# Three layer boundaries of a two-block transformer kernel: the last products by column halves, squares summed unscaled, transposes ahead of the last products, high passes ahead of low passes

## The chip, the cores and the metric

The kernel runs on one core of a Trainium2 chip. The metric is device microseconds (us) of one execution. Five engines each work through their own list of instructions in order and meet at semaphores: TensorE (PE, matrix products and transposes into PSUM), VectorE (DVE), ScalarE (ACT), GpSimd (POOL) and SyncE (SP, which issues transfers).

## The reference

Two blocks run one after the other on 256 tokens of width 1024, in float32.

```python
u  = rms_norm(x, ln1) * (1 + scale1) + shift1        # block 1
x  = x + gate1 * (merged @ w_o)                      # convolution and state-space mixers
u2 = rms_norm(x, ln2) * (1 + scale2) + shift2
x  = x + gate2 * (square(relu(u2 @ w_up)) @ w_down)
x  = rms_norm(x, final_norm)
h  = rms(x, ln1_g) * (1 + sc1) + sh1                 # block 2
x  = x + g1 * (attention(h) @ w_out)
h2 = rms(x, ln2_g) * (1 + sc2) + sh2
x  = x + g2 * ((silu(h2 @ w_gate) * (h2 @ w_up)) @ w_down)
```

Three times a product into the width 1024 is followed by gate, residual, normalization over the whole row, scale and shift, and the next product: after `w_o`, after `w_down` of block 1 (there with `final_norm` in between) and after `w_out`. These places are the boundaries b1, b2 and b3.

## The kernel before

Each float32 matrix is held as two parts, high and low (`wh`, `wl` for weights, `hs`, `ls` for activations), and a product is the sum of three passes: high by high, high by low, low by high. Weights come in units of 1 MB, loaded some units ahead; ACT writes the high part (L133), DVE the low part (L141). In the long stages between the boundaries PE runs nearly without a gap. A scheduler orders the instructions there; inside `boundary` the order is that of the code (`tc.manual_schedule`), and a few of the scheduler's instructions are slipped in between.

The tokens are two tiles of 128, `t` = 0 and 1. A boundary has these steps, for each tile. `last(t, i)` are the last two units (`i`) of the product, 12 products of 512 columns each, into two PSUM banks, one for each half `c` of the columns. `res` multiplies by the gate (`rtmp`), adds to the residual `x`, and at b2 multiplies by `final_norm` (`xq`); `sq` is a sum of squares on ACT (two at b2); `stat` forms the mean on DVE in small steps and the power -1/2 on POOL (`rs`); `norm` scales each half (`xn`). `tf` transposes 8 blocks of 128 by 128 on PE into two PSUM banks of four blocks each; `mod` applies scale and shift to each block, four by ACT and four by DVE, into `f`; `high` and `low` (ACT, DVE) split pairs of blocks. `first(t, i)` are the products of the first two units of the next layer with these parts. `split_by_hand` splits one more weight unit in quarters.

The PSUM tile `tf` has two buffers (`aux`), which `hidt`, the transposes that follow b1 and b3, also use. Where ACT and DVE both read blocks of one bank, the program makes each read wait for the one before it.

After b2 the stage of attention begins: `fgps` and `fgsum` are two small products, `dk` is the next weight unit, and `qt` transposes `qn`, the normalized `dq`, whose chain runs ACT, DVE, POOL (`qkr`, L234), DVE (L1348).

## Time and profile before

| | |
|---|---|
| median of 3 runs | 936.97 us (936.65 to 939.52) |
| the profiled execution | 938.36 us, of which its trace spans 935.9 us |
| PE busy | 898.3 us of the span (96%) |
| DVE, ACT, POOL busy | 732.7, 516.9, 75.7 us |
| b1, b2, b3 in the trace | about 401 to 430, 590 to 625, 729 to 758 us |

The profiled execution is 1.39 us above the median of the runs. Rows of the trace give a start, a duration, an engine, a line, the operation with the tiles written and read, and in brackets the idle time before it and what ended that.

### The profile page before, as it was taken

The page shows a single profiled execution, that of the slowest core. Times are in us where ns is not written, and L with a number is a line of the kernel's source. Part 1 is how long each engine was busy: PE and PEld are TensorE (multiplying, and loading weights), DVE is VectorE, ACT ScalarE, POOL GpSimd, SP SyncE. Part 2 cuts the span into 40 slices and gives each one's busy share as a digit, 9 for nine tenths or more (in the row PEclk, how much of TensorE's full clock was granted, in tenths as well). Part 3 has the DMA queues.
Part 4 walks back from the last instruction along what each step waited for, and adds up shares of the span by engine and source line. Part 5 has one row for each costly group of instructions (what it writes and reads, how often), then busy time and mean ns, then how long its engine had stood idle before and what let it go on. Part 6 is the DMA issues. An engine that isn't in the chain of part 4 may idle for free.

```text
span 935.9 us, 14692 instructions
## 1 busy us (share of the span) xinstructions
PE 898.3 (96%) x5820; PEld 792.6 (85%) x5820; DVE 732.7 (78%) x1091; ACT 516.9 (55%) x901; POOL 75.7 (8%) x98
## 2 busy tenths in 40 slices
PE   5999999999999999989999999889899899999997
PEld 4899999999999999879888888667676698888886
DVE  4779779899989986669798898776878586666663
ACT  5465476676767754437444455465566475555441
POOL 5000000100110000010100100122220100000001
PEclk9999999999999999999999999989999999999999
DMA  9977999677857674556699799346333265655511
GB/s 340 353 254 243 316 354 321 203 262 257 309 195 263 225 250 155 181 202 231 233 356 350 252 360 342 126 134 212 136 118 124 87 212 193 188 203 187 188 46 45
DMA packets 124345, 210.72 MB, mean 225 GB/s; under 512 B 5581, under 2 KB 96045, under 8 KB 119029
## 3 DMA queue, kind: packets, MB, share of 16 engines
q1 hardware_dynamic: 121700, 202.16, 62.1%
q0 software_dynamic: 2496, 7.61, 2.4%
q8 instruction: 45, 0.74, 0.3%
q14 instruction: 24, 0.19, 0.1%
q10 hardware_dynamic: 80, 0.02, 0.0%
HBM read 208.67 MB, written 1.11 MB: 224 GB/s over the span
## 4 chain that ended last, share of the span: by engine, by line
PE 47%; DVE 4%; ACT 2%; POOL 1%; issue 1%; DVEq 0%; ACTq 0%; POOLq 0%
PE tmacc L1009 17%; PE up L682 5%; PE upj L682 3%; PE up L685 2%; PE gatej L682 2%; PE up2j L682 2%; PE gate L682 2%; PE upj L685 1%; POOL qkr L234 1%; PE fv L1273 1%; PE gatej L685 1%; PE gate L685 1%; PE up2j L685 1%; PE dq L1273 1%; PE gu L1189 1%; PE up L1189 1%
## 5 line engine op out<-in xcount | busy, mean ns | idle before, releaser
L141 DVE TENSOR_TENSOR wl<-raw,wh 128x1024 fp32r<-128x1024 f32 x264 | 315.3, 1220 | 75.4 <-ACT wh L133 75.3
L133 ACT ACTIVATE wh<-raw 128x1024 fp32r<-128x1024 f32 x264 | 267.3, 1052 | 138.8 <-PE tmacc L1009 18.4
L283 DVE SCALAR_TENSOR_TENSOR adaacc<-raw,ccol,adaacc 128x1024 f32<-128x1024 f32 x80 | 99.6, 1277 | 5.2 <-DMA raw<-in_w_ada_dram 5.2
L1009 PE MATMUL tmacc<-wh,hidh 128*128 128x512 f32 x216 | 67.2, 392 | 0.0
L1009 PE MATMUL tmacc<-wl,hidh 128*128 128x512 f32 x216 | 66.7, 390 | 0.0
L1009 PE MATMUL tmacc<-wh,hidl 128*128 128x512 f32 x216 | 66.6, 390 | 0.0
L682 PE MATMUL up<-fs,wh 128*128 128x512 f32 x192 | 48.6, 393 | 0.0
L1009 PEld LDWEIGHTS tmacc<-wl,hidh 128*128 128x128 f32 x216 | 40.6, 188 | 8.7
L1009 PEld LDWEIGHTS tmacc<-wh,hidl 128*128 128x128 f32 x216 | 40.5, 188 | 8.7
L1009 PEld LDWEIGHTS tmacc<-wh,hidh 128*128 128x128 f32 x216 | 38.8, 189 | 7.3 <-issue 0.8
L682 PEld LDWEIGHTS up<-fs,wh 128*128 128x128 f32 x192 | 35.1, 188 | 8.4 <-issue 1.7
L817 DVE SCALAR_TENSOR_TENSOR cv<-xc,cwx,cv 128x255 f32<-128x255 f32 (+2 forms) x96 | 39.6, 478 | 0.3 <-ACT cv L812 0.2
L926 PE MATMUL ssmacc<-yl,wh 128*128 128x256 f32 x128 | 35.7, 284 | 0.1
L926 PE MATMUL ssmacc<-yh,wl 128*128 128x256 f32 x128 | 35.7, 284 | 0.0
L926 PE MATMUL ssmacc<-yh,wh 128*128 128x256 f32 x128 | 34.4, 288 | 1.1 <-ACT yh L894 1.1
L701 PE MATMUL xs<-u,wh 128*128 128x256 f32 x256 | 34.6, 286 | 0.0
L701 PE MATMUL z<-u,wh 128*128 128x256 f32 x256 | 34.3, 284 | 0.0
L701 PE MATMUL gl<-u,wh 128*128 128x256 f32 x256 | 33.8, 284 | 0.0
L701 PEld LDWEIGHTS gl<-u,wh 128*128 128x128 f32 x256 | 31.9, 192 | 0.3 <-issue 0.3
L701 PEld LDWEIGHTS z<-u,wh 128*128 128x128 f32 x256 | 32.1, 192 | 0.0
L701 PEld LDWEIGHTS xs<-u,wh 128*128 128x128 f32 x256 | 32.0, 192 | 0.0
L682 PE MATMUL upj<-fs,wh 128*128 128x512 f32 x112 | 28.1, 393 | 0.0
(438 smaller groups left out, 1964.5 us busy)
## 6 DMA issues: line engine op xcount, KB each, us to landing
raw<-in_w_in_dram SPq DMA_DIRECT2D x50, 1024.0 KB, 5.1
raw<-in_w_ada_dram SPq DMA_DIRECT2D x40, 1024.0 KB, 5.6
raw<-in_w_up_dram SPq DMA_DIRECT2D x27, 1024.0 KB, 5.4
raw<-in_w_down_dram SPq DMA_DIRECT2D x27, 1024.0 KB, 6.1
raw<-in_w_gate_dram SPq DMA_DIRECT2D x11, 1024.0 KB, 4.9
a<-in_w_ada_dram SPq DMA_DIRECT2D x16, 512.0 KB, 9.5
raw<-in_w_ssm_out_dram SPq DMA_DIRECT2D x8, 1024.0 KB, 5.0
raw<-in_w_in_dram SPq DMA_DIRECT2D x8, 768.0 KB, 9.3
```

Source lines behind the costliest of these rows:

```text
L133: act(wh[:, sl, :], v[:, sl, :], AF.Copy)
L141: e_.tensor_tensor(wl[:, sl, :], v[:, sl, :], wh[:, sl, :].bitcast(F32), op=ALU.subtract)
L234: pool.tensor_tensor(rs, ms, nhalf[:, :n], op=ALU.pow)
L283: dve.scalar_tensor_tensor(t[:, sl], v[:, 0, sl], ada_c[-1][:, 8 * blk + k : 8 * blk + k + 1], t[:, sl], op0=ALU.mult, op1=ALU.add)
L682: pe.matmul(ps[j].rearrange("p i c -> p (i c)"), wh[:, k, js], xq[k // 2][:, k % 2].rearrange("p i c -> p (i c)"), start=(k == 0), stop=Fa ...
L685: pe.matmul(ps[j][:, 0, :], wl[:, k, js], xq[k // 2][:, k % 2, 0, :], start=False, stop=(k == nk - 1), skip_group_check=True)
L701: pe.matmul(ps[:, j, :], ww[:, k, j * 128 : (j + 1) * 128], xx(k), start=(k == 0 and n == 0), stop=(k == nk - 1 and n == 2))
L817: dve.scalar_tensor_tensor(v[:, j, d:], ps[:, j, : S - d], wc, v[:, j, d:], op0=ALU.mult, op1=ALU.add)
L926: pe.matmul(ssm_acc[q][:, j, :], l_, r_, start=(i == 0 and j == 0 and k == 0 and n == 0), stop=(i == 7 and j == 1 and k == 1 and n == 2), ...
L1009: pe.matmul(accs[t][c], l_, ww[:, kk, c * 512 : (c + 1) * 512], start=(first and kk == 0 and n == 0), stop=(last and kk == 1 and n == 2))
L1189: pe.matmul(ps[:, i * 256 : (i + 1) * 256], l_, ww[:, k, :], start=(i == 0 and k == 0 and n == 0), stop=(i == 1 and k == 7 and n == 2), sk ...
L1273: pe.matmul(ps[t], l_, ww[:, k, :], start=(kk == 0 and n == 0), stop=(kk == 7 and n == 2))
```

## The change

The two last units are computed by column halves: first half 0 of both units, then half 1, and for tile 1 the last 6 products (`last(1, 1, 1)`) come after the transposes of tile 0. Each half's residual and squares follow its products. The sums of squares are no longer divided by 1024; the factor moves into `norm`, and each half has a `stat` step of its own. In `mods` the first two blocks are written by ACT as high parts straight from PSUM, and by DVE as `f`; the other six go as before; all `high` steps come here, and the `low` steps later. `first` is divided into its two high passes and its low pass, and for each tile the high passes of both units come before the low passes. `final` moves behind the split by hand.

```diff
-    def tm_unit(w, accs, xh, xl, k0, first, last, ts=(0, 1)):
...
-                    for c in range(2):
+                    for c in cs:
                         pe.matmul(accs[t][c], l_, ww[:, kk, c * 512 : (c + 1) * 512],
                                   start=(first and kk == 0 and n == 0), stop=(last and kk == 1 and n == 2))
...
         def sq(t, c):
             sl = slice(c * 512, (c + 1) * 512)
-            s1[t].append(square_sum(x[:, t, sl], "s1"))
-            if fnb is not None:
-                s2[t].append(square_sum(srcs[t][:, sl], "s2"))
...
-        def stat(t):
-            m = mean_eps(s1[t], "m")
-            ms[t] = m
-            if fnb is not None:
-                e0, e1, m = tiny(1, "e0"), tiny(1, "e1"), tiny(1, "me")
-                dve.tensor_scalar(e0, ms[t], EPS, None, op0=ALU.mult)
-                dve.tensor_scalar(e1, s2[t][0], 1.0 / D, e0, op0=ALU.mult, op1=ALU.add)
-                dve.tensor_scalar(m, s2[t][1], 1.0 / D, e1, op0=ALU.mult, op1=ALU.add)
-            rss[t] = tiny(1, "rs")
-            pool.tensor_tensor(rss[t], m, nhalf[:, :1], op=ALU.pow)
...
+            for v, s in ((x[:, t, :], s1), (srcs[t], s2))[: 1 if fnb is None else 2]:
+                junk = cur["b"].tile([128, 512], F32, tag="junk", name="junk", bufs=1)
+                act(junk, v[:, sl], AF.Square, accum_out=s[t][:, c : c + 1])
+
+        def stat(t, c):
+
+
+            a, b = s1[t][:, c : c + 1], s2[t][:, c : c + 1]
+            if c == 0:
+                rss[t] = tiny(3, "rs")
+                r1s[t] = tiny(2, "r1")
+                dve.tensor_scalar(r1s[t][:, 0:1], a, D * EPS, None, op0=ALU.add)
+                if fnb is not None:
+                    dve.tensor_scalar(rss[t][:, 0:1], a, EPS, D * EPS * EPS, op0=ALU.mult, op1=ALU.add)
+                    dve.tensor_tensor(rss[t][:, 0:1], rss[t][:, 0:1], b, op=ALU.add)
+            else:
+                if fnb is None:
+                    dve.tensor_tensor(rss[t][:, 1:2], a, r1s[t][:, 0:1], op=ALU.add)
+                else:
+                    dve.scalar_tensor_tensor(rss[t][:, 0:1], a, EPS, rss[t][:, 0:1], op0=ALU.mult, op1=ALU.add)
+                    dve.tensor_tensor(rss[t][:, 1:2], b, rss[t][:, 0:1], op=ALU.add)
+                pool.tensor_tensor(rss[t][:, 2:3], rss[t][:, 1:2], nhalf[:, :1], op=ALU.pow)
...
-            dve.tensor_scalar(xns[t][:, sl], srcs[t][:, sl], rss[t], None, op0=ALU.mult)
+            dve.tensor_scalar(xns[t][:, sl], srcs[t][:, sl], rss[t][:, 2:3], D ** 0.5, op0=ALU.mult, op1=ALU.mult)
...
+        def mod(t, kk, ps, eng, dst=None):
+            dst = (fs if dst is None else dst)[kk // 2][:, kk % 2, t * 128 : (t + 1) * 128]
+            src = ps[kk // 4][:, kk % 4, :]
+            if eng is dve:
+                dve.tensor_scalar(dst, src, g[:, kk : kk + 1], sh[:, kk : kk + 1], op0=ALU.mult, op1=ALU.add)
+            else:
+                act(dst, src, AF.Identity, scale=g[:, kk : kk + 1], bias=sh[:, kk : kk + 1])
...
-        def low(t, p):
+        def low(t, *ps_):
             ts = slice(t * 128, (t + 1) * 128)
-            dve.tensor_tensor(ls[p][:, :, ts], fs[p][:, :, ts], hs[p][:, :, ts].bitcast(F32), op=ALU.subtract)
-
-        def feature(t, ps, between):
-            for p in range(4):
-                mod(t, p, ps[p // 2])
-                if p > 0:
+            for p in ps_:
+                dve.tensor_tensor(ls[p][:, :, ts], fs[p][:, :, ts], hs[p][:, :, ts].bitcast(F32), op=ALU.subtract)
+
+        def mods(t, ps):
+
+            for j in range(2):
+                mod(t, j, ps, act, hs)
+                mod(t, j, ps, dve)
+            for p in (1, 2, 3):
+                mod(t, 2 * p + 1, ps, act)
+                mod(t, 2 * p, ps, dve)
+                if p > 1:
                     high(t, p - 1)
-                if p > 1:
-                    low(t, p - 2)
-                    between(p - 2)
             high(t, 3)
-            low(t, 2)
-            low(t, 3)
...
         with tc.manual_schedule():
-            last(0, 0)
-            last(0, 1)
-            res(0, 0)
-            res(0, 1)
+            last(0, 0, 0)
+            last(0, 1, 0)
+            for step in range(3):
+                res(0, 0, step)
             sq(0, 0)
+            stat(0, 0)
+            last(0, 0, 1)
+            last(0, 1, 1)
+            for step in range(3):
+                res(0, 1, step)
             sq(0, 1)
-            stat(0)
-            last(1, 0)
-            last(1, 1)
+            stat(0, 1)
+            last(1, 0, 0)
+            last(1, 1, 0)
+            last(1, 0, 1)
+            res(1, 0, 0)
             norm(0, 0)
             norm(0, 1)
-            res(1, 0)
+            for step in (1, 2):
+                res(1, 0, step)
             ps = [tf(0, kq) for kq in range(2)]
-            feature(0, ps, mid)
+            last(1, 1, 1)
+            mods(0, ps)
+            first(0, 0, False, u)
+            first(0, 1, False, u)
+            sq(1, 0)
+            stat(1, 0)
+            for step in range(3):
+                res(1, 1, step)
             sq(1, 1)
-            stat(1)
-            final(0)
-            first(0, 0, u)
+            low(0, 0, 1)
+            stat(1, 1)
+            low(0, 2)
             norm(1, 0)
             norm(1, 1)
-            n0 = 2 if fnb is not None else 0
-            first(0, 1, u, 0, n0)
+            low(0, 3)
+            first(0, 0, True, u)
             ps = [tf(1, kq) for kq in range(2)]
-            first(0, 1, u, n0, 8)
-            feature(1, ps, lambda i: None)
+            first(0, 1, True, u)
+            mods(1, ps)
+            first(1, 0, False, u)
+            first(1, 1, False, u)
             f2 = split_by_hand()
+            low(1, 0, 1)
             for q in range(4):
                 f2(q, None)
+                if q == 0:
+                    low(1, 2, 3)
                 f2(q, dve)
+            final(0)
             final(1)
             if blk == 0:
                 ccol2 = const.tile([128, 16], F32, name="ccol2")
                 dve.tensor_copy(ccol2, ccol)
                 ada_c.append(ccol2)
-            first(1, 0, u)
+            first(1, 0, True, u)
             more = extra[0](fs) if extra else None
-            first(1, 1, u)
+            first(1, 1, True, u)
             if extra:
                 extra[1](more)
...
-    def tm_first(w, i, ps, u, t, k0, k1):
+    def passes(low, lh, ll, wh, wl):
+
+        return ((2, ll, wh),) if low else ((0, lh, wh), (1, lh, wl))
+
+    def tm_first(w, i, ps, u, t, low):
 
         wh, wl = w
-        for k in range(k0, k1):
+        for k in range(8):
             lh, ll = (xk(v)(k)[:, t * 128 : (t + 1) * 128] for v in u)
-            for n, (l_, ww) in enumerate(((lh, wh), (lh, wl), (ll, wh))):
+            for n, l_, ww in passes(low, lh, ll, wh, wl):
                 pe.matmul(ps[:, i * 256 : (i + 1) * 256], l_, ww[:, k, :], start=(i == 0 and k == 0 and n == 0),
                           stop=(i == 1 and k == 7 and n == 2), skip_group_check=True)
...
-    def qkv_half(ps, w, kb, t, u, k0=0, k1=4):
+    def qkv_half(ps, w, kb, t, u, *lows):
         wh, wl = w
-        for k in range(k0, min(k1, 4)):
-            kk = 4 * kb + k
-            lh, ll = (xk(v)(kk)[:, t * 128 : (t + 1) * 128] for v in u)
-            for n, (l_, ww) in enumerate(((lh, wh), (lh, wl), (ll, wh))):
-                pe.matmul(ps[t], l_, ww[:, k, :], start=(kk == 0 and n == 0), stop=(kk == 7 and n == 2))
...
+        for low in lows:
+            for k in range(4):
+                kk = 4 * kb + k
+                lh, ll = (xk(v)(kk)[:, t * 128 : (t + 1) * 128] for v in u)
+                for n, l_, ww in passes(low, lh, ll, wh, wl):
+                    pe.matmul(ps[t], l_, ww[:, k, :], start=(kk == 0 and n == 0), stop=(kk == 7 and n == 2))
...
-                    qkv_half(ps, w, kb, t, (u3h, u3l))
+                    qkv_half(ps, w, kb, t, (u3h, u3l), False, True)
```

The first place is DVE at b1, between the blocks of tile 0 and the last low part of tile 0. `f<-tf` are blocks, `fs<-f,fs` low parts, `rtmp` and `x` the residual of tile 1, half 1, `xn` the normalized tile 1. Before:

```order
L1064 TENSOR_TENSOR rtmp<-tmacc,gate 128x512 [waits PE_49]
L1105 TENSOR_SCALAR f<-tf,g_4814,adacol_2313 128x128 [waits Activation_49] x3
L1113 TENSOR_TENSOR fs<-f,fs 128x2x128 [waits DVE_49]
L1105 TENSOR_SCALAR f<-tf,g_4814,adacol_2313 128x128 [waits Activation_49]
L1113 TENSOR_TENSOR fs<-f,fs 128x2x128 [waits DVE_49]
L1064 TENSOR_TENSOR rtmp<-tmacc,gate 128x512
L1065 TENSOR_TENSOR x<-rtmp,x 128x512 [waits DVE_49]
L1113 TENSOR_TENSOR fs<-f,fs 128x2x128 [waits Activation_49] x2
L1046 TENSOR_SCALAR m_4931<-s_4923 128x1
L1047 TENSOR_SCALAR m_4932<-s_4929,m_4931 128x1 [waits DVE_49,Activation_49]
L1090 TENSOR_SCALAR xn<-x,rs 128x512 [waits Pool_49]
```

The same place on DVE in the changed kernel:

```order
L1108 TENSOR_SCALAR f<-tf,g_4814,adacol_2313 128x128 [waits Activation_49] x5
L1080 TENSOR_SCALAR r_4955<-s_4883 128x1 [waits Activation_49]
L1061 TENSOR_TENSOR rtmp<-tmacc,gate 128x512 [waits PE_49]
L1063 TENSOR_TENSOR x<-rtmp,x 128x512 [waits DVE_49]
L1119 TENSOR_TENSOR fs<-f,fs 128x2x128 x2
L1086 TENSOR_TENSOR rs<-s_4883,r_4955 128x1 [waits Activation_49]
L1119 TENSOR_TENSOR fs<-f,fs 128x2x128
L1096 TENSOR_SCALAR xn<-x,rs 128x512 [waits Pool_49]
L1096 TENSOR_SCALAR xn<-x,rs 128x512 [waits DVE_49]
L1119 TENSOR_TENSOR fs<-f,fs 128x2x128
```

There are five blocks now and not four, the low parts stand behind two waits for ACT, and the last one behind the wait for POOL.

The second place is PE at b1, around the transposes of tile 1. `up_4796` is tile 0's product, `up_4797` tile 1's. Before:

```order
L1189 MATMUL up_4796<-wh,fs 128x256
L1095 MATMUL tf<-ident,xn 128x128 [waits DVE_49]
L1095 MATMUL tf<-ident,xn 128x128 x3
L1095 MATMUL tf<-ident,xn 128x128 [waits DVE_49]
L1095 MATMUL tf<-ident,xn 128x128 x3
L1189 MATMUL up_4796<-wh,fs 128x256
L1189 MATMUL up_4796<-wl,fs 128x256
L1189 MATMUL up_4796<-wh,fs 128x256 x2
```

PE in the changed kernel, from the last low products ahead of the transposes on:

```order
L1214 MATMUL up_4796<-wh,fs 128x256 [waits DVE_49]
L1214 MATMUL up_4796<-wh,fs 128x256
L1101 MATMUL tf<-ident,xn 128x128 x8
L1214 MATMUL up_4796<-wh,fs 128x256 x8
L1214 MATMUL up_4797<-wh,fs 128x256 [waits Activation_49]
L1214 MATMUL up_4797<-wl,fs 128x256
L1214 MATMUL up_4797<-wh,fs 128x256 [waits Activation_49]
L1214 MATMUL up_4797<-wl,fs 128x256
L1236 MATMUL hidt<-ident,f 128x128 [waits DVE_49]
L1236 MATMUL hidt<-ident,f 128x128 x3
L1214 MATMUL up_4797<-wh,fs 128x256 [waits Activation_49]
```

Behind the transposes of tile 1 stood 24 products of tile 0, which need nothing of tile 1; now 8 stand there. `hidt` of tile 0, which stood behind all products of the boundary, stands among the first ones of tile 1.

The third place is PE in the second unit of `dk`, after b2. Before:

```order
L1356 MATMUL qt<-ident,qn 128x128 [waits DVE_49,PE_49,Activation_49]
L1356 MATMUL qt<-ident,qn 128x128 x3
L1273 MATMUL dk<-wh,fs 128x512
L1273 MATMUL dk<-wl,fs 128x512
L1273 MATMUL dk<-wh,fs 128x512 x2
L1273 MATMUL dk<-wl,fs 128x512
L1273 MATMUL dk<-wh,fs 128x512
L1356 MATMUL qt<-ident,qn 128x128 [waits DVE_49,Activation_49]
L1356 MATMUL qt<-ident,qn 128x128 x3
```

PE there in the changed kernel:

```order
L1382 MATMUL qt<-ident,qn 128x128 [waits DVE_49,PE_49,Activation_49]
L1382 MATMUL qt<-ident,qn 128x128 x3
L1299 MATMUL dk<-wh,fs 128x512
L1299 MATMUL dk<-wl,fs 128x512
L1382 MATMUL qt<-ident,qn 128x128 [waits DVE_49,Activation_49]
L1382 MATMUL qt<-ident,qn 128x128 x3
```

Between the two groups of `qt` there were 6 products, and now there are 2.

## Rows read from the trace of the kernel before

**Rows 1.** The page, part 1: busy us of each engine.

```profile
PE 898.3 (96%) x5820; PEld 792.6 (85%) x5820; DVE 732.7 (78%) x1091; ACT 516.9 (55%) x901; POOL 75.7 (8%) x98
```

**Rows 2.** Waits of PE: waiter, awaited; us in total, times, longest.

```profile
PE tf L1095 <- DVE xn L1090: 4.7, 4, 2.8
```

**Rows 3.** Timeline of PE at b1: start, duration, operation, count.

```profile
410.43 1.07 PE L1009 MATMUL tmacc<-wh,m 128*128 128x512 f32 x4
...
412.25 1.03 PE L1095 MATMUL tf<-ident,xn 128*128 128x128 f32 x8
414.64 0.39 PE L1189 MATMUL up<-wh,fs 128*128 128x256 f32 x1 [1.35 <-ACT fs L1109]
414.87 0.28 PE L1189 MATMUL up<-wl,fs 128*128 128x256 f32 x1
...
420.26 1.09 PE L1095 MATMUL tf<-ident,xn 128*128 128x128 f32 x8 [0.44 <-DVE xn L1090]
421.11 0.37 PE L1189 MATMUL up<-wh,fs 128*128 128x256 f32 x1
...
429.83 0.60 PE L1211 MATMUL hidt<-ident,f 128*128 128x128 f32 x4
```

**Rows 4.** Timelines of ACT, DVE and POOL at b1.

```profile
412.89 0.46 ACT L1103 ACTIVATE f<-tf,adacol,g 128x128 f32<-128x128 f32 x1 [2.54 <-PE tf L1095]
413.83 0.46 ACT L1103 ACTIVATE f<-tf,adacol,g 128x128 f32<-128x128 f32 x1 [0.48 <-DVE f L1105]
414.19 0.41 ACT L1109 ACTIVATE fs<-f 128x256 fp32r<-128x256 f32 x1
...
418.08 0.63 ACT L1040 ACTIVATE junk<-x 128x512 f32<-128x512 f32 x1 [0.97 <-DVE x L1065]
...
413.38 0.41 DVE L1105 TENSOR_SCALAR f<-tf,g,adacol 128x128 f32<-128x128 f32 x1 [0.47 <-ACT f L1103]
...
416.58 0.68 DVE L1064 TENSOR_TENSOR rtmp<-tmacc,gate 128x512 f32<-128x512 f32 x1
417.29 0.69 DVE L1065 TENSOR_TENSOR x<-rtmp,x 128x512 f32<-128x512 f32 x1
417.90 0.76 DVE L1113 TENSOR_TENSOR fs<-f,fs 128x256 fp32r<-128x256 f32 x2
...
418.83 0.21 DVE L1047 TENSOR_SCALAR m<-s,m 128x1 f32<-128x1 f32 x1
419.72 0.88 DVE L1090 TENSOR_SCALAR xn<-x,rs 128x512 f32<-128x512 f32 x2 [0.68 <-POOL rs L1084]
...
419.13 0.56 POOL L1084 TENSOR_TENSOR rs<-m,nhalf 128x1 f32<-128x1 f32 x1 [4.82 <-DVE m L1047]
```

**Rows 5.** Timeline of PE at b2.

```profile
599.74 0.62 PE L1009 MATMUL tmacc<-wh,hidh 128*128 128x512 f32 x2
...
602.30 1.06 PE L1095 MATMUL tf<-ident,xn 128*128 128x128 f32 x8 [1.04 <-DVE xn L1090]
604.72 0.50 PE L1273 MATMUL dq<-wh,fs 128*128 128x512 f32 x1 [1.35 <-ACT fs L1109]
...
613.20 1.97 PE L1095 MATMUL tf<-ident,xn 128*128 128x128 f32 x8 [2.76 <-DVE xn L1090]
...
619.50 0.62 PE L1273 MATMUL dq<-wh,fs 128*128 128x512 f32 x2
...
625.09 0.53 PE L725 MATMUL fgsum<-fold,fgpart 128*128 128x32 f32 x4
```

**Rows 6.** Windows of 1 us at b2; the eighth figure is the granted clock.

```profile
613.00:614.00 1.00, 0.80 (x4) 0.81 (x5) 1.00 (x3) 0.00 (x0) 0.81 (x2) 0.50 0.01 4
...
620.00:621.00 1.00, 1.00 (x6) 0.72 (x4) 1.00 (x3) 1.00 (x2) 0.00 (x0) 1.00 0.00 0
```

**Rows 7.** Timelines of PE and POOL after b2.

```profile
634.62 0.63 PE L1356 MATMUL qt<-ident,qn 128*128 128x128 f32 x4 [1.50 <-DVE fg L744]
...
631.19 2.56 POOL L234 TENSOR_TENSOR qkr<-qkm,nhalf 128x8 f32<-128x8 f32 x1 [0.97 <-DVE qkm L233]
```

More of the change, by code (lines that the diff above doesn't have):

```diff
@@ L999, in tile_hybrid_blocks, with tm_unit @@
     ph.close()
-    def tm_unit(w, accs, xh, xl, k0, first, last, ts=(0, 1)):
+    def tm_unit(w, accs, xh, xl, k0, first, last, ts=(0, 1), cs=(0, 1)):
         wh, wl = w
@@ L1055, in boundary, with res @@
         hs, ls, hl = zip(*[halves("fs") for _ in range(4)])
-        srcs, xns, s1, s2, ms, rss = [None, None], [None, None], [[], []], [[], []], [None, None], [None, None]
-        def res(t, c):
+        srcs, xns, s1, s2, rss, r1s = ([None, None] for _ in range(6))
+        tmps = {}
+        def res(t, c, step):
             sl = slice(c * 512, (c + 1) * 512)
             e_ = pool if c == 0 and t == 1 else dve
-            if c == 0:
-                srcs[t] = x[:, t, :] if fnb is None else cur["b"].tile([128, D], F32, tag="xq", name="xq", bufs=2)
-            tmp = cur["b"].tile([128, 512], F32, tag="rtmp", name="rtmp", bufs=2)
-            dve.tensor_tensor(tmp, accs[t][c], gate[:, sl], op=ALU.mult)
-            e_.tensor_tensor(x[:, t, sl], tmp, x[:, t, sl], op=ALU.add)
-            if fnb is not None:
+            if step == 0:
+                if c == 0:
+                    srcs[t] = x[:, t, :] if fnb is None else cur["b"].tile([128, D], F32, tag="xq", name="xq", bufs=2)
+                    s1[t], s2[t] = tiny(2, "s1"), tiny(2, "s2")
+                tmps[t, c] = cur["b"].tile([128, 512], F32, tag="rtmp", name="rtmp", bufs=2)
+                dve.tensor_tensor(tmps[t, c], accs[t][c], gate[:, sl], op=ALU.mult)
+            elif step == 1:
+                e_.tensor_tensor(x[:, t, sl], tmps[t, c], x[:, t, sl], op=ALU.add)
+            elif fnb is not None:
                 e_.tensor_tensor(srcs[t][:, sl], x[:, t, sl], fnb[:, sl], op=ALU.mult)
@@ L1128, in final @@
             if fnb is not None:
-                r1 = tiny(1, "r1")
-                pool.tensor_tensor(r1, ms[t], nhalf[:, :1], op=ALU.pow)
-                dve.tensor_scalar(x[:, t, :], srcs[t], r1, None, op0=ALU.mult)
+                a, r = s1[t][:, 1:2], r1s[t]
+                pool.tensor_tensor(r[:, 0:1], a, r[:, 0:1], op=ALU.add)
+                pool.tensor_tensor(r[:, 1:2], r[:, 0:1], nhalf[:, :1], op=ALU.pow)
+                dve.tensor_scalar(x[:, t, :], srcs[t], r[:, 1:2], D ** 0.5, op0=ALU.mult, op1=ALU.mult)
@@ L1197, in around, with fn @@
         drain()
-        def fn(t, i, u, k0=0, k1=8):
+        def fn(t, i, low, u):
             if len(w3) <= i:
                 w3.append(take())
-            first(w3[i], t, i, u, k0, k1)
-        return (lambda t, i: last(w2[i], t, i)), fn
+            first(w3[i], t, i, u, low)
+        return (lambda t, i, c: last(w2[i], t, i, c)), fn
     def to_hid(f, t, his):
@@ L1545, in tile_hybrid_blocks @@
     gu_ps = [ps_mm.tile([128, 512], F32, tag="mm", name="gu0") for _ in range(2)]
-    fns = around(lambda w, t, i: tm_unit(w, accs, xk(mx_h), xk(mx_l), 2 * i, False, i == 1, (t,)),
-                 lambda w, t, i, u, k0, k1: tm_first(w, i, gu_ps[t], u, t, k0, k1))
+    fns = around(lambda w, t, i, c: tm_unit(w, accs, xk(mx_h), xk(mx_l), 2 * i, False, i == 1, (t,), (c,)),
+                 lambda w, t, i, u, low: tm_first(w, i, gu_ps[t], u, t, low))
     _, u4h, u4l, u4q = boundary(fns[0], gate, x, 1, 2, col("ln2g2", 8), fns[1])
```

28 lines of the change are left out of this document (5 added, 23 removed).

## The prediction

> **What bounds the kernel now.** The page's first part comes first: PE is busy for 96% of the span [rows 1], so a change on another engine counts only where PE waits for it. The view of waits says where: the longest of the waits that belong to a boundary stand ahead of `tf`, four times, 4.7 us in all [rows 2]. I then read the timelines of b1 and b2 and take what PE loses there as time passed less work done, with start-to-start times of back-to-back rows: 8 products of 512 columns take 1.82 us (410.43 to 412.25), .2267 each; 8 transposes .85; the 72 products of 256 columns that end b1 take 8.72, .121 each [rows 3].
>
> At b1, 410.43 to 429.83 is 19.40 us, and holds 8 products of 512 (1.81), 16 transposes (1.70) and 96 products of 256 (11.62), together 15.1. PE loses 4.3 us [rows 3]. At b2, 599.74 to 625.09 is 25.35, and holds 6 + 48 products of 512 (12.24), 16 transposes and 16 `fgps` (1.0): 14.9, so 10.4 are lost [rows 5]. A part of these 10.4 is the clock: the granted clock is 0.50 (1.2 GHz) when PE comes back from 2.76 us without work, and 1.00 (2.4 GHz) again by 620 [rows 5, 6]. From 613.20 to 619.50 eight transposes and eleven products took 6.30 where full rate makes .85 + 2.49 = 3.34 [rows 5]. Not all of the 2.96 would come back at full rate: tile 0's first product began 2.42 after its transposes [rows 5], so with only 6 products (1.36) behind tile 1's, waits of about .9 would show. I take 2 us as the clock's net cost. b3, which has b1's steps, I take as b1.
>
> **The change at b1, step by step.** Latencies, start to start unless said [rows 3, 4]: transposes to ACT's first block .64; a block of ACT to the next of DVE .49, DVE's to ACT's .45; `rtmp` to `x` .71; `x` to its square .79; square to the mean .75; mean to POOL .30; POOL to `xn` .59; `xn` to its second half .40. A high part takes .41, two low parts .76. The product behind the first one after a stall starts .23 later and not .12 [rows 3], so each stall costs .11 more than it lasts.
>
> *What it removes.* The transposes start about 410.9 and not at 412.25, since 6 of the 12 last products (1.36) move behind them and tile 0's `xn` is there by then: with half 0 summed early, only half 1's square, one mean, POOL and `xn` are left behind its residual. The products end at 410.9 + .85 + 1.36 = 413.1. The first four high products run at once, from the two blocks that ACT writes as high parts: 413.6. The 1.35 in front of the first product goes.
>
> *What it adds.* Blocks 0 and 1 are now read from the bank by ACT and by DVE. The six reads of that bank take turns: ACT at T = 411.5, DVE T + .49, ACT + .94, DVE + 1.43, ACT + 1.88, DVE + 2.37. The next high part needs the last of them, so it begins at about T + 2.8 and ends at 414.8. PE, idle since 413.6, waits 1.24, and .13 for the next.
>
> *What it moves.* All low parts stand on DVE behind the residual of tile 1's half 1, and this behind a wait for ACT's square of half 0 (order, first place), which stands on ACT behind all high parts. So: last high part begins 415.6, square 416.0, DVE free 416.8, `rtmp` 416.8, `x` 417.5, first low part 418.1. PE has 28 high products left at 414.8 (3.4 and .24 of stalls), and comes to the low ones at 418.5: waits of .09, then .36. Behind `x`: square 418.25, mean 419.0, POOL 419.25, `xn` 419.85 and 420.26, last low part 420.67 to 421.08. It stands behind `xn`, so PE waits 1.24 for it. Queued behind that product are the transposes of tile 1 (421.5), behind them only 8 products (.97) where 24 (2.9) stood (order, second place). The second tile's blocks then show: .03 for the second high block, .96 for `hidt`, .23 and .10 for high parts.
>
> *Sum at b1.* Waits 1.24 + .13 + .09 + .36 + 1.24 + .03 + .96 + .23 + .10 = 4.4, nine stalls 1.0: 5.4 lost, against 4.3. **+1.1.** At b3 the same, with the steps of `gu` in place of `hidt`'s: **+1.1**.
>
> A rule bears on the alternation of ACT and DVE. The Trainium skill, PSUM — Partial Sum Buffer, section "PSUM bank collisions raise a hardware error", says that two engines must not touch one bank in the same partitions at once, reads included, so the program has to order them. The trace agrees: ACT 412.89, DVE 413.38, ACT 413.83, each begins as the one before ends [rows 4]. Were the two engines free to read together, the high part would be there .94 earlier and the sum at b1 would be about +.2.
>
> **At b2** the same order is longer by the second square, two means and `xq`. By the same durations PE waits 1.11 for `xn`, .79 for a high part, 2.48 for the first low part, .82 for tile 1's `xn`, 1.25 for its high part: 6.45, with stalls 7.0. Laid out in the same way the old order loses 7.7; from the trace it is 10.4 - 2 = 8.4. The gain without the clock lies between -.7 and -1.4; I take **-1.0**. What comes from: `final(0)` no longer stands on DVE ahead of tile 1's `xn`. The clock: a gap of 2.76 let it fall, gaps of 1.35 and 1.04 did not [rows 5]. The new longest gap, 2.48, is nearest to the first, so I let the clock cost what it cost; if it stays up, a further -2.
>
> **At `dk`** between the two groups of `qt` stand 2 products where 6 stood (order, third place). The second group waited 1.50 [rows 7] for a chain that follows the end of `dq` through POOL's `qkr` (631.19 + 2.56 = 633.75). With 4 x .2267 less in front, and the chain where it was behind `dq`, the wait is 2.4: **+.9**. The four products come later and hide nothing there.
>
> The unscaled sums trade one tiny DVE step for one or two others beside ACT's squares: nothing on PE; without that cover .2 us each [rows 4]. `split_by_hand` and `final` move behind `low`; neither is waited for by PE, since the unit is needed only after the boundary: nothing, at most the .4 of one DVE step at each place.
>
> **Sum.** +1.1 - 1.0 + .9 + 1.1 = +2.1 to the profiled execution's 938.36: 940.5. That execution lies 1.39 above the median of the runs, so the forecast is 936.97 + 2.1 = **939.1 us**.
>
> **The rivals.**
> A, the sum: 45%, 937.7 to 940.2. The lower end takes -1.4 at b2 and half the price of the bank reads (-.5 at b1 and b3 each), the upper one -.7 at b2 and the .4 at two places.
> B, the clock stays at 2.4 GHz over b2, since the longest gap there shrinks: 937.1, 18%. For it: 2.48 is under 2.76. Against: they are close.
> C, the clock falls at the `dk` gap too, which grows from 1.50 to 2.4: 2 us more as at b2, 941.1, 14%. The Trainium skill, TensorE: Matmul & The Clock Gate, Part 1, calls the throttled state the default and says that activity releases it; 0.50 after the gap and 1.00 after work agree [rows 6]. By that rule every longer gap is a risk to the clock.
> D, the other side: the 32 high products in a row cover all that stands on ACT and DVE, so that low parts and second tile bring no waits. Then b1 and b3 keep 1.24 + .13 and two stalls, 1.6 against 4.3, -2.7 each, and b2, half of its 8.4, -4: with +.9, 928.5. What decides is the last low part at b1: it would have to end by about 419.4 and not at 421.1. For it speaks that ACT may do the square before the high parts' waits end, against it DVE's order. 13%.
> E, stages further on lose: the split of the unit by hand now comes later in DVE's queue, and the units behind it with it; one wait as long as the longest in front of `tf` [rows 2] is 2.8: 941.9, 10%.
>
> **How the numbers follow.** About 0.3%, 2.8 us, is what a measurement of this kernel can tell from no change: under 934.2 is faster, over 939.8 slower. A puts a quarter of its 45% above 939.8; with C and E that makes .35 slower. D is faster, with a little of B: .15. The rest, .50, is the same. The range leaves out D and, above, C and E together: 934.5 to 943.
>
> **What would show it.** Right: at b1 `tf` starts ahead of the last 6 products, some 1.4 us earlier against the start of the boundary, with no wait; a wait of `up` for ACT's `fs` of about 1.2, one of 1.2 for DVE's last low part just ahead of `tf` of tile 1, and about 1 for `hidt`; at b2 about 2.5 for the first low part, 0.8 to 1.1 for each `xn`; at `qt` 2.4. Wrong: no wait ahead of the low products (D), clock 1.00 all over b2 (B), 0.50 behind `qt` (C), new waits of PE in later stages (E).

## The result and the profile after

The changed kernel takes 942.9 us (median of 6 runs, 941.5 to 944.41), the kernel before 937.14 (6 runs, 936.65 to 939.52): the ratio is 1.0053, with a 95% interval from 1.0043 to 1.0064. It is slower by 5.8 us. That is inside the range given, by .1 us, but far above the point of 939.1 and above the point of every rival. The profiled execution took 942.48, and its trace spans 940.8 us, 4.9 more than the trace before; only these 4.9 can be placed by the rows below.

First the view of PE's waits in the changed kernel (awaited; us in total, times, longest); it answers to [rows 2] and to the waits in [rows 3, 5, 7].

```profile
PE tf L1101 <- DVE xn L1096: 4.9, 5, 2.1
...
PE qt L1382 <- DVE fg L740: 2.2, 1, 2.2
PE hidt L1236 <- DVE f L1108: 2.2, 2, 1.1
PE dq L1299 <- ACT fs L1114: 1.7, 1, 1.7
PE dq L1299 <- DVE fs L1119: 1.5, 1, 1.5
PE up L1214 <- DVE fs L1119: 1.3, 2, 1.2
PE gu L1214 <- DVE fs L1119: 1.3, 2, 1.2
```

The waits of 1.35 for ACT's first high part are gone, and `hidt`, the low parts and `qt` wait as the prediction had it. What it did not have is in the first row: `tf` still waits 4.9 us, of which the prediction had 1.9, at b2.

A table by stage, from starts of PE's rows in both traces (`y3t` lies ahead of b1, L682 is the first product behind it, `fgsum` ends b2, the first `fo` ends the stages up to attention's output, the last `tmacc` group lies at the end):

| stretch | before | after | difference | foretold |
|---|---|---|---|---|
| `y3t` to L682 (b1) | 382.52 to 430.18 | 382.91 to 431.98 | +1.4 | +1.1 |
| L682 to `fgsum` (b2) | to 625.09 | to 625.93 | -1.0 | -1.0 |
| `fgsum` to `fo` (`dk` and after) | to 717.91 | to 719.40 | +.65 | +.9 |
| `fo` to the last `tmacc` (b3) | to 929.60 | to 934.48 | +3.4 | +1.1 |

With the .4 by which `y3t` already stood later (it lies between 382.5 and 383.9 in all twelve traces) this is the 4.9 us between the spans. The totals of three of the four places came out within .3; b3 did not.

**Why `tf` waits.** First two rows at b1 of the kernel before, tile 0's `xn` and POOL's addition behind it (start, duration, operation, count, and the idle time before it):

```profile
411.28 0.89 DVE L1090 TENSOR_SCALAR xn<-x,rs 128x512 f32<-128x512 f32 x2 [0.69 <-POOL rs L1084]
...
413.05 1.26 POOL L1065 TENSOR_TENSOR x<-rtmp,x 128x512 f32<-128x512 f32 x1 [1.80 <-issue]
```

Then the rows of DVE, POOL and PE at b1 and at b2 of the changed kernel:

```profile
410.76 1.89 DVE L1096 TENSOR_SCALAR xn<-x,rs 128x512 f32<-128x512 f32 x2
410.93 1.44 POOL L1063 TENSOR_TENSOR x<-rtmp,x 128x512 f32<-128x512 f32 x1 [0.21 <-issue]
411.30 0.66 PE L1101 MATMUL tf<-ident,xn 128*128 128x128 f32 x4
412.71 0.66 PE L1101 MATMUL tf<-ident,xn 128*128 128x128 f32 x4 [0.75 <-DVE xn L1096]
...
601.95 1.26 POOL L1063 TENSOR_TENSOR x<-rtmp,x 128x512 f32<-128x512 f32 x1
601.96 2.94 DVE L1096 TENSOR_SCALAR xn<-xq,rs 128x512 f32<-128x512 f32 x2
603.29 1.33 POOL L1065 TENSOR_TENSOR xq<-x,fnb 128x512 f32<-128x512 f32 x1
603.64 0.94 PE L1101 MATMUL tf<-ident,xn 128*128 128x128 f32 x4 [2.07 <-DVE xn L1096]
```

The pair of `xn` took .89 before; now it takes 1.89 at b1 and b3 and 2.94 at b2. Read together, the rows say that DVE's `xn` does not get on while POOL adds: at b1 one half is caught by one addition, at b2 each half by one of POOL's two operations. Run 1 tests this. The change put `rtmp` of tile 1 ahead of `xn`, so POOL's work starts together with `xn`; in the kernel before it came behind it.

**b3.** PE's rows behind tile 1's transposes, and windows of 1 us there (the eighth figure is the granted clock):

```profile
755.02 0.44 PE L1236 MATMUL hidt<-ident,gu 128*128 128x128 f32 x2 [1.10 <-DVE f L1108]
...
756.59 0.39 PE L1214 MATMUL gu<-wh,fs 128*128 128x256 f32 x1 [0.38 <-ACT fs L1114]
...
757.18 0.41 PE L1214 MATMUL gu<-wh,fs 128*128 128x256 f32 x1
...
760.59 0.39 PE L1214 MATMUL gu<-wh,fs 128*128 128x256 f32 x1
```

```profile
756.00:757.00 1.00, 0.62 (x5) 0.42 (x5) 1.00 (x4) 0.82 (x3) 0.00 (x0) 1.00 0.00 0
758.00:759.00 1.00, 1.00 (x7) 1.00 (x6) 1.00 (x3) 1.00 (x3) 0.00 (x0) 0.50 0.00 0
760.00:761.00 1.00, 1.00 (x7) 1.00 (x7) 1.00 (x2) 1.00 (x2) 0.00 (x0) 0.59 0.00 0
```

The clock falls to 0.50 (1.2 GHz) while PE works, behind three waits of 1.16, 1.10 and .38 us. The 16 products from 757.18 to 760.59 take 3.41 where 16 x .121 make 1.9: 1.5 us. The kernel before had no such fall at b3 in its trace. At b1 of the change, behind waits of 1.16 and 1.13, the clock stayed at 1.00 in this execution.

At b2 the clock fell too, but sooner and for a shorter time, from 604 to 607.9 and not from 612 to 619 as in [rows 6]:

```profile
604.00:605.00 1.00, 0.59 (x3) 0.18 (x1) 0.91 (x1) 0.38 (x1) 0.62 (x1) 0.50 0.00 0
606.00:607.00 1.00, 1.00 (x4) 0.81 (x4) 0.42 (x2) 0.52 (x3) 0.00 (x0) 0.50 0.00 0
```

What the clock lost at b3 it thus lost less at b2: the two traces have the same mean granted clock, 0.993.

### The profile page after: what moved, and what is told of

Its sections match the earlier page's. It is cut to its first block, busy times and chain, and to the rows that moved or that the text cites. A ratio compares the mean times of both kernels' runs of the same rounds, so it can differ in the third digit from the quotient of the medians.

```text
span 940.8 us, 14698 instructions
## 1 busy us (share of the span) xinstructions
PE 900.8 (96%) x5820; PEld 793.5 (84%) x5820; DVE 737.1 (78%) x1097; ACT 519.0 (55%) x901; POOL 75.8 (8%) x100
## 3 DMA queue, kind: packets, MB, share of 16 engines
HBM read 208.67 MB, written 1.11 MB: 223 GB/s over the span
## 4 chain that ended last, share of the span: by engine, by line
PE 44%; DVE 6%; ACT 3%; POOL 1%; issue 1%; DMA 0%; ACTq 0%; DVEq 0%
PE tmacc L1009 17%; PE up L682 5%; PE upj L682 3%; PE up L685 2%; PE gatej L682 2%; PE up2j L682 2%; PE gate L682 2%; PE upj L685 1%; DVE wl L141 1%; PE fv L1299 1%; PE gatej L685 1%; PE gate L685 1%; PE up2j L685 1%; POOL qkr L234 1%; PE fk L1299 1%
## 5 line engine op out<-in xcount | busy, mean ns | idle before, releaser
L682 PE MATMUL up<-fs,wh 128*128 128x512 f32 x192 | 48.1, 392 | 0.0
L682 PEld LDWEIGHTS up<-fs,wh 128*128 128x128 f32 x192 | 35.1, 188 | 8.4 <-ACT wh L133 0.8
L682 PE MATMUL upj<-fs,wh 128*128 128x512 f32 x112 | 28.1, 393 | 0.0
```

What stands on the lines that cost most here:

```text
L682: pe.matmul(ps[j].rearrange("p i c -> p (i c)"), wh[:, k, js], xq[k // 2][:, k % 2].rearrange("p i c -> p (i c)"), start=(k == 0), stop=Fa ...
```

## The experiments

Ten kernels ran, each timed against the kernel before on the same chip (runs 1 to 4, 5 to 8, 9 and 10; its median there: 938.68, 937.52 and 937.18). Between groups, differences below are those of the ratios, times 938 us; by the intervals, each is known to 1.5 to 2.5 us. Each execution also has a mean granted clock. As an estimate, .001 of it is worth at most .94 us of a span of 940, namely if PE works all that time.

| kernel | median us | ratio to before, 95% interval |
|---|---|---|
| the change | 942.9 | 1.0053 (1.0043 to 1.0064) |
| 1 `xn` ahead of the residual | 945.19 | 1.0064 (1.0044 to 1.0085) |
| 2 tiny step late | 940.23 | 1.0016 (0.9999 to 1.0033) |
| 3 waits filled | 943.6 | 1.0054 (1.0036 to 1.0071) |
| 4 first part alone | 932.25 | 0.9931 (0.9915 to 0.9947) |
| 5 edits 1 and 2 | 936.57 | 0.9996 (0.9981 to 1.001) |
| 6 as 5, blocks once | 932.38 | 0.9936 (0.9916 to 0.9957) |
| 7 as 4, transposes behind | 934.32 | 0.996 (0.9946 to 0.9974) |
| 8 before, gap filled | 937.75 | 1.0002 (0.999 to 1.0014) |
| 9 the change, blocks once | 938.95 | 1.0013 (1.0003 to 1.0024) |
| 10 as 4, blocks twice | 936.09 | 0.9982 (0.9968 to 0.9996) |

### 1. xn ahead of the residual

```diff
-            res(1, 0, 0)
             norm(0, 0)
             norm(0, 1)
-            for step in (1, 2):
+            for step in range(3):
                 res(1, 0, step)
```

> The changed kernel with one edit: the two halves of xn of tile 0 stand ahead of the residual of tile 1's half 0 (DVE's rtmp, then POOL's adds). Theory P (DVE's xn and POOL's adds hold each other up): the pair of xn, which took 1.89, 2.94 and 1.89 us at b1, b2, b3, takes about .9 at each; the wait of tf ahead of its second bank goes at b1 and b3 (.75 and .79), and at b2 the transposes start about 1.1 earlier. At b1 and b3 the time that PE gets back there is lost again in front of the third high product, which waits for the chain of blocks that starts with the first bank, so 0 there; b2 gains 1.1 to 1.5, and with a wait of tf of 1 us instead of 2.1 the clock stays up around 605. Whole: 1 to 2 us less than the changed kernel, ratio to before about 1.004. Rival Q (xn is long for a reason of its own, such as its semaphores or the second factor): the pairs keep their length, and the time does not move.

The rows at b2, and two windows of the places where the clock fell:

```profile
604.68 0.88 DVE L1096 TENSOR_SCALAR xn<-xq,rs 128x512 f32<-128x512 f32 x2 [0.69 <-POOL rs L1090]
605.31 1.06 PE L1101 MATMUL tf<-ident,xn 128*128 128x128 f32 x8 [1.00 <-DVE xn L1096]
606.24 1.30 POOL L1063 TENSOR_TENSOR x<-rtmp,x 128x512 f32<-128x512 f32 x1 [1.60 <-DVE rtmp L1061]
```

```profile
424.00:425.00 1.00, 1.00 (x7) 1.00 (x6) 0.17 (x1) 0.46 (x1) 0.00 (x0) 0.50 0.00 0
762.00:763.00 1.00, 1.00 (x6) 1.00 (x6) 1.00 (x4) 1.00 (x4) 0.00 (x0) 0.50 0.00 0
```

The mechanism is shown: `xn` takes .88 at b1, b2 and b3, and `tf` waits 1.0 at b2 and not at all at b1 and b3. The time did not follow: the ratio is 1.0064 where 1.004 was expected, and the change has 1.0053. In the profiled execution (946.99, the longest of its six) the clock fell at 423, 614, 638, 754 and 761, and at `fk`, the products of attention behind PE's wait of 3.6 us, as in every kernel but run 2; b1 alone took 1.7 us more than in the change. Over the six executions the mean granted clock is .990, in the change .993: by the estimate above up to 3 us, more than the 1 to 2 that were expected to be won. So the clock can have taken the gain, but a gain in time by this edit alone is not shown. On top of run 2 it may bring 1.9 us (run 5, ratio 1.0016 to 0.9996), with intervals that overlap.

### 2. The tiny step late

```diff
             sq(1, 0)
-            stat(1, 0)
             for step in range(3):
                 res(1, 1, step)
+            stat(1, 0)
             sq(1, 1)
```

> The changed kernel with one edit: on DVE the tiny step of tile 1's half 0 (r, rs), which waits for ACT's square, stands behind the residual of tile 1's half 1 and not ahead of it. Theory D (the queue of DVE sets the end of the low parts): DVE's waits of 1.1 us at b1 and b3 and of 1.1 and .6 at b2 go, the residual, the low parts and xn of tile 1 come as much earlier, and PE's waits ahead of the low products (1.3 at b1, 1.3 at b3, 1.5 at b2) shrink to .2 or less. At b3 the granted clock, which fell to 0.50 at 757 to 761 behind these waits and cost 1.5 us, stays at 1.00. 4 to 5.5 us less than the changed kernel: at or just above the kernel before, ratio 0.999 to 1.002. Rival: the low parts come earlier, but PE then waits as long for tile 1's transposes and blocks, so under 1 us is won.

In the changed kernel DVE stood still in front of the tiny step, and PE for the last low part (b1):

```profile
417.24 0.15 DVE L1080 TENSOR_SCALAR r<-s 128x1 f32<-128x1 f32 x1 [1.10 <-ACT junk L1071]
...
421.79 0.51 PE L1214 MATMUL up<-wh,fs 128*128 128x256 f32 x2 [1.16 <-DVE fs L1119]
```

DVE at b1 in this run, between the last block and the low parts:

```profile
415.47 0.41 DVE L1108 TENSOR_SCALAR f<-tf,g,adacol 128x128 f32<-128x128 f32 x1 [0.53 <-ACT f L1110]
415.79 0.68 DVE L1061 TENSOR_TENSOR rtmp<-tmacc,gate 128x512 f32<-128x512 f32 x1
416.51 0.69 DVE L1063 TENSOR_TENSOR x<-rtmp,x 128x512 f32<-128x512 f32 x1
417.12 0.15 DVE L1080 TENSOR_SCALAR r<-s 128x1 f32<-128x1 f32 x1
417.18 0.75 DVE L1119 TENSOR_TENSOR fs<-f,fs 128x256 fp32r<-128x256 f32 x2
```

DVE no longer stands still for 1.1 us behind its last block, and PE's waits for low parts fall from 1.3 to .5 at b1 and b3 and vanish at b2, where PE also came later, at a granted clock of .50 from 603 to 609. By the ratios this is 3.5 us (1.0053 to 1.0016), a little less than expected. The clock did not bring it: its mean over the executions is .993 in both. In the profiled execution (936.03, the shortest of its twelve) the clock stays at 1.00 at b3. A step of .15 us that waits for another engine cost this, since a residual, the low parts and `xn` were queued behind it.

### 3. The waits filled

```diff
-            ps = [tf(0, kq) for kq in range(2)]
+            p0 = tile4()
+            if fnb is not None:
+                fill(p0, 16)
+            ps = [tf(0, 0, p0), tf(0, 1)]
...
-            first(0, 0, True, u)
-            ps = [tf(1, kq) for kq in range(2)]
+            p0 = tile4()
+            first(0, 0, True, u, lambda k: fill(p0, 10) if fnb is None and k == 6 else None)
+            ps = [tf(1, 0, p0), tf(1, 1)]
```

`fill` transposes `ident` into a buffer that the real transposes overwrite.

> The changed kernel with transposes added whose result nobody reads: 16 at b2 in front of tile 0's transposes, and 10 at b1 and b3 in front of the last four low products of tile 0's first unit, where PE stood still. Every other instruction keeps its order. Theory C (PE's idle stretches let the clock fall): the windows at 604 to 607 and at 757 to 761 show 1.00 and not 0.50, the 16 products at b3 that took 3.4 us take 1.9; some 1.5 us at b3 and up to .5 at b2 are won, 1.5 to 2 in all, ratio about 1.0035. Rival: the clock falls at these places for another reason (what ACT and DVE do, or the power drawn then), the windows stay at 0.50, and the time is the same or, where a fill ends late, up to .5 longer.

A window at b3 in this run:

```profile
760.00:761.00 1.00, 1.00 (x6) 1.00 (x6) 1.00 (x3) 1.00 (x2) 0.00 (x0) 0.50 0.00 0
```

The theory fell in this form: the long wait ahead of the last low products was filled, and the clock fell at b3 all the same, with only the waits for `hidt` (1.11) and a high part (.38) left behind the fill. At b2 it no longer fell at 604, but at 615, behind a wait for the first low part that had grown from 1.48 to 2.17, and then at 635, behind the `qt` gap. The time did not move.

### 4. The first part alone

Column halves, unscaled sums, the transposes ahead and `final` late, edits 1 and 2 with them; the block order, `first` with its three passes in turn and the products behind tile 1's transposes are as in the kernel before.

```diff
-            mods(0, ps)
-            first(0, 0, False, u)
-            first(0, 1, False, u)
-            sq(1, 0)
+            feature(0, ps, mid)
             stat(1, 0)
-            for step in range(3):
-                res(1, 1, step)
             sq(1, 1)
-            low(0, 0, 1)
             stat(1, 1)
-            low(0, 2)
+            first(0, 0, None, u)
             norm(1, 0)
             norm(1, 1)
-            low(0, 3)
-            first(0, 0, True, u)
+            n0 = 2 if fnb is not None else 0
+            first(0, 1, None, u, 0, n0)
             ps = [tf(1, kq) for kq in range(2)]
...
+            first(0, 1, None, u, n0, 8)
+            feature(1, ps, lambda i: None)
```

`feature` makes blocks, high and low parts in turn, and `mid` puts tile 1's residual in between.

> One part of the change alone: column halves, unscaled sums, tile 0's transposes ahead of the last 6 products and final behind the split, with xn ahead of tile 1's residual; the order of blocks, high and low parts and of the first products (high, high, low for each block) and the 24 or 18 products behind tile 1's transposes are those of the kernel before. Theory S (the first half of the change gains, the high passes ahead of the low ones lose it): the wait for the first high part (1.35 at each boundary in the kernel before) goes or shrinks under .3, tile 1 waits as before, at b2 the old 2.8 us in front of tf shrink by about .7 for final: 1.4 at b1 and b3 and 2 to 4 at b2, that is 4 to 6 us less than the kernel before, ratio about 0.995. Rival: tile 1's chain ends the boundary whatever tile 0 does, so PE waits as much longer in front of tile 1's transposes, and the time is that of the kernel before, ratio 1.000.

The boundary's rows of PE at b1, which answer to [rows 3]:

```profile
411.32 1.09 PE L1101 MATMUL tf<-ident,xn 128*128 128x128 f32 x8
...
414.90 0.51 PE L1222 MATMUL up<-wh,fs 128*128 128x256 f32 x2 [0.62 <-DVE fs L1119]
417.50 0.50 PE L1222 MATMUL up<-wh,fs 128*128 128x256 f32 x2 [0.69 <-DVE fs L1119]
419.34 1.09 PE L1101 MATMUL tf<-ident,xn 128*128 128x128 f32 x8 [0.40 <-DVE xn L1096]
```

The wait of 1.35 is gone and no new one stands in its place. At b2 the clock stayed at 1.00 throughout, and the stretch from L682 to `fgsum` is 4.9 us shorter than before; b1 and b3 are 1.1 and 1.4 shorter. Behind b2 the clock fell at 629, after a `qt` gap of 1.97, and the stretch from `fgsum` to `fo` is 1.6 longer. This version beats both kernels, by 6.4 us the one before. Not all of that is waits saved: its mean granted clock over the executions is .997, that of the kernel before on this chip .992, by the estimate above up to 4.5 us.

### 5 and 6. Both edits, and then each block once

Run 5 has the edits of runs 1 and 2 on the change. Run 6 has besides:

```diff
-            for j in range(2):
-                mod(t, j, ps, act, hs)
-                mod(t, j, ps, dve)
-            for p in (1, 2, 3):
+            for p in range(4):
                 mod(t, 2 * p + 1, ps, act)
                 mod(t, 2 * p, ps, dve)
-                if p > 1:
+                if p > 0:
                     high(t, p - 1)
```

> The changed kernel with the edits of both earlier runs on it: xn of tile 0 ahead of tile 1's residual, and the tiny step of tile 1's half 0 behind the residual of half 1. What it still has against the run with the first part of the change alone is the second part: blocks 0 and 1 written twice, the high passes ahead of the low ones, and 8 products behind tile 1's transposes. Theory S: this second part costs by itself, by PE's waits of 1.0 for the third high product and 1.1 for hidt at b1 and b3, 2 to 2.5 at b2, and by the clock that falls behind them: 938 to 940 us, 6 to 8 more than that run. Rival: that run owed its time to these two edits alone, and this one takes 932 to 934 as well.

> As the run with both edits, but each block of the transposes is read once, by ACT or DVE in turn as in the kernel before, and the high parts of blocks 0 and 1 are made from f. Theory (the six reads of the first bank in turn delay the next high part): the third high product no longer waits 1.0, the waits for high parts sum to .6 or less at b1 and b3 and 1 us less at b2: 1.5 to 3 us less than the run with both edits. Rival: what is won at the high parts is waited for at the low parts, which keep their time since DVE's queue ends with tile 1's residual: the same time within 0.5 us.

ACT at b1 from the first block on, and PE's wait, in run 5:

```profile
411.81 0.46 ACT L1110 ACTIVATE fs<-tf,adacol,g 128x128 fp32r<-128x128 f32 x1 [2.12 <-PE tf L1101]
412.75 0.46 ACT L1110 ACTIVATE fs<-tf,adacol,g 128x128 fp32r<-128x128 f32 x1 [0.48 <-DVE f L1108]
...
414.62 0.42 ACT L1114 ACTIVATE fs<-f 128x256 fp32r<-128x256 f32 x1
...
415.09 0.38 PE L1213 MATMUL up<-wh,fs 128*128 128x256 f32 x1 [1.02 <-ACT fs L1114]
```

And in run 6, where the high part of 414.70 is the one that stands at 414.62 above (blocks 2 and 3):

```profile
412.76 0.46 ACT L1110 ACTIVATE f<-tf,adacol,g 128x128 f32<-128x128 f32 x1 [2.12 <-PE tf L1101]
...
414.05 0.41 ACT L1114 ACTIVATE fs<-f 128x256 fp32r<-128x256 f32 x1
...
414.70 0.41 ACT L1114 ACTIVATE fs<-f 128x256 fp32r<-128x256 f32 x1
```

From the first block to that high part it is 2.81 with blocks written twice and 1.94 with blocks written once: .87, two reads of the bank more in the line. PE's wait of 1.0 becomes three of at most .4. The time falls by 4.2 us by the medians (5.6 by the ratios), more than expected. Run 5, at 936.6, lies below the 938 to 940 expected, but by the ratios 6.1 above run 4: the second part of the change costs by itself, and by run 6 this is the double writing. Run 6, with all high passes first, is level with run 4, so the order of the passes by itself costs nothing that can be told.

### 7. Transposes behind the last products

The edit is shown against run 4.

```diff
+            last(1, 1, 1)
             norm(0, 0)
             norm(0, 1)
...
             ps = [tf(0, kq) for kq in range(2)]
-            last(1, 1, 1)
```

> The first part of the change alone, with one thing taken back: tile 0's transposes stand behind the last 6 products again; column halves, half sums and unscaled sums stay. Theory (the transposes ahead bring the gain): tile 0's blocks start 1.36 us later at b1 and b3, PE waits 1.3 for the first high part again, and the time is 3 to 4 us above the run with that part, 935 to 936. Rival (the halves and the shorter chain to xn bring it): xn stands earlier anyway and the time stays within 1 us of 932.3.

PE's waits in this run:

```profile
PE up L1222 <- ACT fs L1114: 1.4, 1, 1.4
PE dq L1307 <- ACT fs L1114: 1.4, 1, 1.4
PE gu L1222 <- ACT fs L1114: 1.4, 1, 1.4
```

The three waits are back, as expected, but only 2.7 us of them in the time (0.9931 to 0.996, intervals that just touch), where 3 to 4 were expected: PE then waits .8 and not 2.9 us for `xn` in front of `tf`. By this the transposes ahead bring some 2.7 of the 6.4 us of run 4.

### 8. The kernel before with its gap at b2 filled

```diff
-            ps = [tf(1, kq) for kq in range(2)]
+            p0 = aux("tf").rearrange("p (k c) -> p k c", k=4)
+            for k in range(24 if fnb is not None else 0):
+                pe.transpose(p0[:, k % 4, :], ident, ident)
+            ps = [tf(1, 0, p0), tf(1, 1)]
```

> The kernel before, with 24 transposes whose result nobody reads ahead of tile 1's transposes at b2, where PE stood still for 2.8 us; nothing else is changed. Theory C (the clock falls for want of work in this gap, at a net cost of some 2 us): the windows from 612 to 619 show 1.00, and 1.5 to 2.5 us are won, ratio about 0.998. Rival (the clock falls there for another reason, or what it costs would be waited for anyway): 0.50 stays in the windows, or goes without a gain, ratio 1.000.

Two windows, at b2 and at b3:

```profile
616.00:617.00 1.00, 0.74 (x3) 0.30 (x2) 0.76 (x3) 0.83 (x3) 0.00 (x0) 1.00 0.00 0
743.00:744.00 1.00, 1.00 (x6) 1.00 (x6) 1.00 (x3) 0.92 (x4) 0.00 (x0) 0.50 0.00 0
```

At b2 the theory holds in the profiled execution: the clock stays at 1.00, and the stretch from L682 to `fgsum` is 1.9 us shorter, the price of 2 us that the prediction had. The median did not move. In the profiled execution, the fastest of its twelve, the clock fell at 742 to 745, where it had not fallen in the kernel before; but the stretch from `fo` on is 211.7 us in both, so this fall does not explain the median. What does speak to it is the mean granted clock of all executions, .9934 in the twelve against .9927 in the kernel before on this chip: filling this gap hardly raised it.

### 9 and 10. Blocks once in the change, twice in the first part

Run 9 is the change with the edit of run 6 alone. Run 10 is run 4 with blocks 0 and 1 written twice.

> The changed kernel with one edit: each block of the transposes is read once, as in the kernel before, and the high parts of blocks 0 and 1 are made from f. xn, the tiny step and the order of the passes stay as the change has them. Theory B (writing blocks 0 and 1 twice costs 4.2 us, as between the two runs with both edits): 938 to 940 us, 3 to 5 less than the changed kernel, ratio 1.000 to 1.003. Rival: with xn held up by POOL and DVE waiting for the tiny step the blocks are not what is waited for, and under 1 us is won, ratio 1.005.

> The converse: the first part of the change alone, with blocks 0 and 1 written twice as the change does (by ACT as high parts, by DVE as f), all else as in that run. Theory B: the next high parts come .9 later for tile 0 and tile 1, PE waits as much longer for them at each of the three boundaries, 2 to 4 us more: 934.5 to 936.5, ratio about 0.9975. Rival: in this order low parts and not high parts are waited for, so the time stays within 1 us of 932.3, and double writing hurts only where all high passes come first.

PE's rows at b1 in run 10, to be held against those of run 4:

```profile
415.53 0.51 PE L1225 MATMUL up<-wh,fs 128*128 128x256 f32 x2 [1.50 <-DVE fs L1119]
418.13 0.50 PE L1225 MATMUL up<-wh,fs 128*128 128x256 f32 x2 [0.69 <-DVE fs L1119]
```

Run 9 is 3.8 us less than the change, as expected: the waits of 1.1 for `hidt` are gone, and that for tile 1's high part at b2 falls from 1.66 to .43 and .24. Run 10 is 4.8 us more than run 4, where 2 to 4 were expected. At b1 the wait for the first low part grows from .62 to 1.50, by the .88 of the two reads.

## Why the prediction was right, and where it was off

**The number.** The kernel became slower, as forecast, but by 5.8 us and not by 2.1. That 942.9 still lies inside the range is in part luck: by the prediction's own line of 939.8 it is the slower kernel to which it gave .35, and the room above was made for rivals C and E. Neither came about in the trace: the clock stayed up behind `qt`, and the view of waits has no new wait in a later stage. Steps priced too low took their place.

**The sign and the mechanism.** The low parts behind DVE's wait for ACT, the last one behind `xn`, `hidt` among the first products, and 2 products of `dk` where 6 stood: each is in the waits after, at 1.2, 1.1 and 2.2 (`qt`) where 1.24, .96 and 2.4 were foretold. Rival D (32 high products cover everything) is out: waits ahead of the low products stand in every boundary. Runs 2 and 9 show which of these steps weigh: the tiny step in DVE's queue 3.5 us, the blocks written twice 3.8.

One sign named in advance did not come: PE was to wait 1.24 at b1 for ACT's high part of blocks 2 and 3, and it stood idle .15 there. PE came late to it, for the reason in the next paragraph. With `xn` on time the wait is there, 1.02 in runs 1 and 5, and in run 5 the high part starts 2.81 behind the first block where 2.8 was foretold. So the total of b1, within .3 of its term, is one wait foretold and missing against another that was not foretold.

**The step that failed at tile 0.** "The transposes start about 410.9", with `xn` there by then and no wait. The first bank came as foretold: 411.30, in a trace that stood .39 later already at `y3t`. The second bank came only at 412.71, about 1 us late. I had priced `rtmp` ahead of `xn` and POOL's additions at nothing. By run 1 it is POOL's work that holds `xn` up: .88 without it, 1.89 and 2.94 with it. The Trainium skill, SBUF — State Buffer, section "SBUF: two separate sides", says that DVE in a mode that uses two ports and GpSimd share a pair of ports as an exclusive lock, and that the one that comes second is blocked for the whole instruction. The rows behave in this way: at b2 `xn` began at 601.96, .01 us behind POOL's addition, and the transposes that need its first half began at 603.64, behind the addition's end at 603.21. That `xn` runs in such a mode no run here shows by itself.

**What was mis-sized.** Writing blocks 0 and 1 twice was put at .9 for each of b1 and b3, the wait of PE for one high part of tile 0. Run 10 shows .88 for tile 0 at b1, there ahead of a low part. But tile 1 and b2 pay too: in run 9 the waits of 1.1 for tile 1's `hidt` go, and in run 10 a wait of tile 1 at b2 grows from .39 to 1.56. The three pairs of runs give 3.8, 4.2 and 4.8 us in all.

**b3, +3.4 against +1.1.** 1.5 of the 2.3 us missing are the clock at 757 to 761. Rival C had the clock fall once more, for 2 us, but at the `qt` gap; there it stayed up (2.2 of wait), and it fell at b3. Of the rest, .8, b1 has .3 as well. Another .3 is a high part of tile 1: PE waits .38 for it at b3, and counted from the start of `tf` the product behind it stands 16.01 us on and not 15.67 as at b1. The last .2 was not placed.

**b2, -1.0, was right in sum only, and that is luck.** The wait for tile 0's `xn` was 2.07 and not 1.11, that for the first low part 1.48 and not 2.48, as PE came later to it; the .79 for a high part of tile 0 did not come, and tile 1's was 1.66 and not 1.25. The clock, which was to cost what it had cost, fell at 604 and not at 612, and for a shorter time.

**The clock is not the cause of the 5.8 us.** The mean granted clock of the change's executions lay between 0.992 (944.4 us) and 0.995 (941.6), .993 on average. The kernel before has .992 to .993 in its three groups of 17, 25 and 23 executions, and 0.993 in its profiled execution beside the change; the other five there are on record without a clock. So the clock spreads the times of one kernel, and it fell at other places, but on average it cost the change no more than the kernel before.

**What stays open** is when the clock falls. It fell at b3 and not at b1 of one execution, behind waits of the same kind; filling the longest wait there (run 3) did not hold it, and filling the gap at b2 (run 8) did. Behind the `qt` gap of 2.0 to 2.3 us, rival C's place, it fell in the traces of runs 1, 3, 4 and 5, and not in those of the change and of runs 2, 6, 7, 9 and 10. From `fgsum` to `fo` the traces take 92.7 to 93.5 us where the clock fell once or not at all, and 94.2 to 95.0 in the seven (runs 1, 3 to 7 and 9) where it fell twice or for longer; what decides between them no run shows.

## What to carry to other kernels

Ahead of a chain that ends a stage, look at each engine's queue for the small step that waits for another engine: everything behind it waits as well, and moving a step of .15 us was worth 3.5 us here. Two engines that take turns at one bank pay for every read that is added, in all tiles, so a shortcut that gives one consumer its data sooner by a second read can cost the next consumer more. A change of several parts can be taken apart: this one had a part that, with two small moves, was 6.4 us faster than the kernel before, some of it by the clock, and the others hid it. And a time inside the range does not show that the working was right: here two totals fitted because their errors cancelled.
